# A two-layer decoder on one core: the MLP's second product in seven block products per 512 inner features, with half of the weight sums made in DRAM

## The chip, the core and the metric

The kernel runs on one NeuronCore of a Trainium2 chip. The metric is the device time of one execution in microseconds (us); lower is better. PE is TensorE (PEld its weight loads), DVE VectorE, ACT ScalarE, POOL GpSimd, SP SyncE. SP, ACT and POOL can issue DMAs; here SP issues nearly all of them.

## The reference

Two layers on x of 512 tokens x 1024 features, all in float32. A layer:

```
h = RMSNorm(x); z = h @ W_in                       # 1024 x 5888: attention, retention and gate columns
y = sigmoid(ga) * (attention @ W_a) + sigmoid(gb) * (retention @ W_b)
x = x + y @ W_out                                  # all of this is called mixing below
x = x + relu(RMSNorm(x) @ W_up)^2 @ W_down         # the MLP: 1024 -> 4096 -> 1024
```

A final RMSNorm follows. The change touches the MLP: `up` (512 tokens x 1024 times 1024 x 4096), the square of the ReLU, and `down` (512 x 4096 times 4096 x 1024).

## The kernel before

**Numbers.** Each float32 operand is split into a rounded `hi` (float32r, an ACT copy) and the rest `lo` (a DVE subtraction); a product is three matmuls, hi x hi, hi x lo, lo x hi (`products`, lines 274 to 282). Activations live with features on the 128 partitions and 512 tokens along the row; weights are the stationary operand, 128x128, and 512 tokens (in the pairs below 256) move.

**Weights.** All weights pass in a fixed order of units of 128x1024 (`unit_order`). `load_until` has SP fetch a unit into `raw` (three buffers), `split_until` makes `hi` and `lo` (three buffers each) and `unit` hands a unit out after it has split up to two more and loaded three ahead. So the buffers set the pace: the `hi` of unit i needs the end of unit i-3 on PE.

**MLP.** The first 512 inner features come from a plain `group` of four banks. The other 3584 come from 14 `pair`s of 256 inner features, each with a block scheme of seven products instead of eight (Strassen's, in Winograd's form): inputs are cut by feature half and token half, the sums of input blocks (`sums`) are made once per layer (`sum_input`), the sums of the weight blocks on DVE in `add_part` (four of 128x512 per pair), and a product is 12 matmuls of 256 columns. The banks a, e, b of a pair are chained: ACT copies a into b, b goes on accumulating, and so on. `rms_mlp.value`, the inverse root mean square per token, is multiplied in when a bank is read. z is squared and split to `hi` and `lo`.

**Order in the MLP** (`mlp_sequence`): the group, then two pairs, then in turn a down product and a pair. Inner features come in four quarters of 1024; a down product (`two_chunks`) is 256 output features from one quarter, two banks, 48 matmuls of 512 columns, added to x by DVE (`put_down`). The last quarter is done as a group and chunks, in layer 1 (`end`) in two halves of 256 tokens, so that the final norm of the first half runs beside the second. After layer 0 `put_down` also prepares the next layer's input (`scaled_input` makes `xh` and `xl`, `squared_input` the squares) and stores x to `spill`.

The order of instructions on each engine is made by the language's scheduler, which may move independent instructions past each other; each engine then runs its list strictly in order.

Of the kernel before, what the change touches and what calls it, by code (L numbers as in the profile page):

```python
# [10 lines left out]
F32 = mybir.dt.float32  # L11
# [32 lines left out]
N_IN = 46  # L44
UNIT = 1024
# [3 lines left out]
DELAY = 2  # L49


def unit_order():

    order = [("w_in", i) for i in range(4 + 2 + 8 + 2 + 4 + 2)]
    order += [("w_in", i) for i in range(22, 26)]
    order += [("w_a", i) for i in range(4)]
    order += [("w_in", i) for i in range(26, 42)]
    order += [("w_b", i) for i in range(4)]
    order += [("w_in", i) for i in range(42, 46)]
    order += [("w_b", i) for i in range(4, 8)]  # L60
    order += [("w_out", i) for i in range(8)]
    for what, q, i in mlp_sequence():
        if what == "first":
            order += [("w_up", u) for u in range(4)]
        elif what == "pair":
            order += [("pair", 8 * q + 2 * i, part) for part in range(4)]
        elif what == "down":
            order += [("w_down", 8 * q + 2 * i + u) for u in range(2)]
        else:
            order += [("w_down", 8 * q + u) for u in range(8)]  # L70
    return order


def mlp_sequence():

    seq = [("first", 0, 0), ("pair", 0, 2), ("pair", 0, 3)]
    for q in range(3):
        for i in range(4):  # L80
            seq += [("down", q, i), ("pair", q + 1, i)]
    return seq + [("last", 3, 0)]
# [32 lines left out]
def decoder(ctx, tc, xT, x_first, w_in, w_a, w_b, w_out, w_up, w_down, tables, decay, band, out):  # L115
# [14 lines left out]
    def temp(name="t"):  # L130
        return tmp.tile([P, T], F32, tag="t", name=name)
# [23 lines left out]
    raws, parts, homes = {}, {}, []  # L155
# [6 lines left out]
    def raw_tile():  # L162
        return wpool.tile([P, UNIT], F32, tag="raw", name="raw")

# [7 lines left out]
    def load_until(n):  # L172
        while state["loaded"] < min(n, len(order)):
            i = state["loaded"]
            layer, name, j = order[i][:3]
            if name == "pair":
                load_part(i)
            else:
# [12 lines left out]

    def load_part(i):
        layer, _, j, part = order[i]
        if part == 0:
            raws[i] = raw_tile()
            nc.sync.dma_start(raws[i][:, LEFT], w_up[layer, j][:, LEFT])
            raws[i + 3] = raw_tile()
            nc.sync.dma_start(raws[i + 3], w_up[layer, j + 1])
        elif part == 1:
            raws[i] = big("raw2").rearrange("p a t -> p (a t)")  # L200
            nc.sync.dma_start(raws[i][:, RIGHT], w_up[layer, j][:, RIGHT])

    def add_part(i):
        part = order[i][3]
        if part == 0:
            w2 = raws[i + 3]
            nc.vector.tensor_tensor(raws[i][:, RIGHT], w2[:, RIGHT], w2[:, LEFT], ALU.add)
        elif part == 1:
            w1 = raws[i - 1]
            nc.vector.tensor_tensor(raws[i][:, LEFT], w1[:, RIGHT], w1[:, LEFT], ALU.subtract)  # L210
        elif part == 2:
            raws[i] = big("raw3").rearrange("p a t -> p (a t)")
            w1, w2, z2 = raws[i - 2], raws[i + 1], raws[i - 1]
            nc.vector.tensor_tensor(raws[i][:, LEFT], w1[:, LEFT], w2[:, RIGHT], ALU.subtract)
            nc.vector.tensor_tensor(raws[i][:, RIGHT], z2[:, RIGHT], z2[:, LEFT], ALU.subtract)

    def split_until(n):
        while state["split"] < min(n, len(order)):
            i = state["split"]
            load_until(i + 3)  # L220
            paired = order[i][1] == "pair"
            if paired:
                add_part(i)
            raw = raws[i]
            if homes and i >= len(order) - len(homes):
                home = homes[len(order) - 1 - i]
                hi, lo = (home[:, 2 * a : 2 * a + 2, :].rearrange("p a t -> p (a t)") for a in range(2))
            else:
                hi = wpool.tile([P, UNIT], F32R, tag="hi", name="hi")
                lo = wpool.tile([P, UNIT], F32R, tag="lo", name="lo")  # L230
            for at in (LEFT,) if paired and order[i][3] == 3 else halves(i):
# [5 lines left out]
            raws.pop(i - 3 if paired else i, None)  # L237
# [117 lines left out]

    def square_sum(acc, src, first):
# [46 lines left out]
    def end(layer, uT):  # L403
        homes.extend(slots.four()[0] for _ in range(5))
        units = []
        H = T // 2
        g_last = 2 * DEPTH * KD

        def unit_at(i):
            if len(units) == i:  # L410
                units.append(unit("w_down", layer))
            return units[i]

        def half_products(ps, i, col, moving, at, start, stop):
            hi, lo = unit_at(i)
            cols = slice(col, col + P)
            products(ps, [((hi[:, cols], lo[:, cols]), tuple(m[:, at] for m in moving))], start, stop)

        class Half:
            def __init__(self, at):  # L420
                self.at = at
                self.acc = tmp.tile([P, T], F32, tag="acc", name="acc", bufs=1)[:, :H]

            def put(self, c, ps):
                xa = x[:, c, self.at]
                nc.vector.tensor_tensor(xa, xa, ps, ALU.add)
                if c == 0:
                    nc.scalar.activation(self.acc, xa, AF.Square)
                else:
                    sq = temp("sq")[:, :H]  # L430
                    nc.scalar.activation(sq, xa, AF.Square)
                    if c < KD - 1:
                        nc.vector.tensor_tensor(self.acc, self.acc, sq, ALU.add)
                    else:
                        self.last = sq
                nc.scalar.activation(xa, xa, AF.Copy, scale=gain[:, g_last + c : g_last + c + 1])

            def sums(self, ps, src, start):
                nc.tensor.matmul(ps, f32(ones), src, start=start, stop=not start)

            def gemm(self, meanwhile=None):
                banks = [bank(ps_mm, "mm")[:, :H] for _ in range(4)]
                for k in range(KD):
                    for c, ps in enumerate(banks):
                        half_products(ps, k // 2, (k % 2) * T + c * P, uT[k], self.at, k == 0, k == KD - 1)
                    if k == 1 and meanwhile:
                        meanwhile()
                for c, ps in enumerate(banks):
                    self.put(c, ps)
                for c in range(4, KD):  # L450
                    ps = bank(ps_mm, "mm")[:, :H]
                    for k in range(KD):
                        half_products(ps, c, k * P, uT[k], self.at, k == 0, k == KD - 1)
                    if c == KD - 1:
                        self.ssq = bank(ps_aux, "ssq")[:, :H]
                        self.sums(self.ssq, self.acc, True)
                    self.put(c, ps)

            def finish(self):
                self.sums(self.ssq, self.last, False)  # L460
                rstd = tmp.tile([P, T], F32, tag="rstd", name="rstd", bufs=2)[:, :H]
                nc.scalar.activation(rstd, self.ssq, AF.Sqrt, bias=eps, scale=1.0 / D)
                nc.vector.reciprocal(rstd, rstd)
                for k in range(KD):
                    if k % 2 == 0:
                        o = temp("o").rearrange("p (c t) -> p c t", t=H)
                    nc.vector.tensor_tensor(o[:, k % 2, :], x[:, k, self.at], rstd, ALU.mult)
                    if k in (0, 1, KD - 2, KD - 1):
                        nc.sync.dma_start(out[:, k, self.at], o[:, k % 2, :])
                    elif k % 2:  # L470
                        nc.sync.dma_start(out[:, k - 1 : k + 1, self.at], o)

        first = Half(slice(0, H))
        first.gemm()
        second = Half(slice(H, T))
        second.gemm(first.finish)
        second.finish()


    def layer_body(layer):  # L480
        g_mix, g_mlp = 2 * layer, 2 * layer + 1
        rms_mix, rms_mlp = Rms(g_mix), Rms(g_mlp)
# [94 lines left out]
        def put_q(c):  # L577
# [18 lines left out]
            {0: squares, 1: stats_first} if layer == 0 else {0: rms_mix.prepare, 1: stats},  # L596
# [103 lines left out]
        def gate(dest):  # L700
            def put(ps):
                nc.vector.tensor_tensor(dest, ps, rstd(), ALU.mult)
                nc.scalar.activation(dest, dest, AF.Sigmoid)

            return put
# [3 lines left out]
        def put_gate(c):  # L709
            def put(ps):  # L710
                nc.vector.tensor_tensor(mixed[c], ps, rstd(), ALU.mult)

# [9 lines left out]
        def put_ret(box, h):  # L722
            def put(ps):
# [4 lines left out]
                box[h] = (hi, lo)  # L728

# [524 lines left out]
```

## Time and profile before

| | |
|---|---|
| device time, median of 3 runs | 1511.3 us (1511.27 to 1512.82) |
| span of the profiled execution | 1511.4 us |
| busy in it: PE, PEld, DVE, ACT, POOL | 99%, 86%, 68%, 49%, 0% |
| DMA | 155.10 MB, mean 103 GB/s |
| MLP of layer 0, of layer 1 | about 414 to 751 us, 1161 to 1503 us with the final norm |

The profile is one execution seen by the hardware profiler. Part 1 of its page is the busy time of each engine, part 4 the chain of work that ended last. A group's row reads: line, engine, operation, output <- input, shape, count | busy us, mean ns of one | idle time just before them and what ended it. Matmuls are pipelined: one starts before the last has ended, so the mean of one is longer than the distance between two. A row of the table by stretches reads: from:to, length, then busy us (count) of PE, PEld, DVE, ACT, POOL, then the granted clock of PE, the DMA engines' share and GB/s.

### The profile page before, as it was taken

What the parts mean: (1) busy time and instruction counts of PE and PEld (TensorE: products, weight loads), DVE (VectorE), ACT (ScalarE), POOL (GpSimd) and SP (SyncE); (2) the same over time, 40 slices, a digit from 0 to 9 for tenths busy, and PEclk for the clock granted to TensorE, in tenths of its full rate; (3) what the DMA queues carried; (4) which work ended last, traced back from release to release, by engine and by line L of the source; (5) the groups of instructions that cost most, each with busy time, mean ns of one, the idle gap of its engine ahead of it and who ended that gap; (6) DMA issues with size and microseconds to landing.
All of it is one profiled execution on the core that took longest, in us unless ns stands there. A gap on an engine that the chain in (4) does not pass through costs nothing.

```text
span 1511.4 us, 20498 instructions
## 1 busy us (share of the span) xinstructions
PE 1499.2 (99%) x8080; PEld 1302.2 (86%) x8080; DVE 1026.7 (68%) x1598; ACT 740.1 (49%) x1163; POOL 2.9 (0%) x13
## 2 busy tenths in 40 slices
PE   9999999999999999999999999999999999999997
PEld 7888888888888999989888888888888999889997
DVE  6877668754787666676678765777449866666664
ACT  6656455632564444444455742555327544444452
POOL 0000000000000000000000000000000000000000
PEclk9999999999999999999999999999999999999999
DMA  6422322233223232233442222222342232232331
GB/s 217 123 97 75 98 79 91 70 125 126 98 78 104 98 112 97 93 104 115 165 131 93 84 84 98 82 79 84 126 125 98 85 104 92 99 111 98 103 108 56
DMA packets 52640, 155.10 MB, mean 103 GB/s; under 512 B 6208, under 2 KB 8384, under 8 KB 52544
## 3 DMA queue, kind: packets, MB, share of 16 engines
q1 hardware_dynamic: 52400, 153.54, 30.6%
q8 instruction: 63, 1.03, 0.3%
q14 instruction: 33, 0.27, 0.1%
q10 hardware_dynamic: 144, 0.26, 0.0%
HBM read 146.96 MB, written 4.19 MB: 100 GB/s over the span
## 4 chain that ended last, share of the span: by engine, by line
PE 98%; ACT 1%; DVE 0%; DMA 0%; issue 0%; DVEq 0%
PE mm L280 29%; PE mm L281 29%; PE mm L282 29%; PE rv L280 2%; PE rv L281 2%; PE rv L282 2%; PE score L651 1%; PE pT L616 1%; PE r L281 1%; PE r L282 1%; PE r L280 1%; PE pv L637 0%; PE pv L636 0%; PE ssq L374 0%; PE ret L281 0%; PE ret L282 0%
## 5 line engine op out<-in xcount | busy, mean ns | idle before, releaser
L235 ACT ACTIVATE hi<-raw 128x1024 fp32r<-128x1024 f32 (+1 forms) x313 | 314.6, 1013 | 517.9 <-PE mm L281 430.6
L236 DVE TENSOR_TENSOR lo<-raw,hi 128x1024 fp32r<-128x1024 f32 (+1 forms) x314 | 362.6, 1164 | 162.0 <-ACT hi L235 161.1
L281 PE MATMUL mm<-r,hi 128*128 128x512 f32 (+1 forms) x1136 | 392.5, 346 | 0.0
L280 PE MATMUL mm<-r,hi 128*128 128x512 f32 (+1 forms) x1136 | 389.5, 346 | 1.0 <-ACT mm L1037 1.0
L282 PE MATMUL mm<-r,lo 128*128 128x512 f32 (+1 forms) x1136 | 388.5, 346 | 0.0
L280 PE MATMUL mm<-xh,hi 128*128 128x512 f32 (+1 forms) x1008 | 358.2, 357 | 0.9 <-ACT xh L290 0.9
L281 PE MATMUL mm<-xl,hi 128*128 128x512 f32 (+1 forms) x1008 | 356.8, 356 | 0.0
L282 PE MATMUL mm<-xh,lo 128*128 128x512 f32 (+1 forms) x1008 | 355.4, 356 | 0.0
L280 PEld LDWEIGHTS mm<-r,hi 128*128 128x128 f32 x1136 | 214.8, 189 | 27.8 <-ACT mm L1037 1.4
L281 PEld LDWEIGHTS mm<-r,hi 128*128 128x128 f32 x1136 | 215.3, 189 | 26.3
L282 PEld LDWEIGHTS mm<-r,lo 128*128 128x128 f32 x1136 | 215.0, 189 | 25.7
L280 PEld LDWEIGHTS mm<-xh,hi 128*128 128x128 f32 x1008 | 191.1, 190 | 27.1 <-ACT xh L290 1.6
L281 PEld LDWEIGHTS mm<-xl,hi 128*128 128x128 f32 x1008 | 191.3, 190 | 25.5
L282 PEld LDWEIGHTS mm<-xh,lo 128*128 128x128 f32 x1008 | 191.0, 190 | 25.5
L1064 DVE TENSOR_TENSOR x<-x,mm 128x512 f32<-128x512 f32 x56 | 37.8, 687 | 34.2 <-PE mm L282 34.2
L282 PE MATMUL rv<-hi,xl 128*128 128x512 f32 x128 | 49.8, 389 | 0.0
L281 PE MATMUL rv<-lo,xh 128*128 128x512 f32 x128 | 49.8, 389 | 0.0
L280 PE MATMUL rv<-hi,xh 128*128 128x512 f32 x128 | 49.4, 391 | 0.0
L281 PE MATMUL mm<-ulo,hi 128*128 128x512 f32 (+1 forms) x128 | 46.3, 363 | 0.0
L280 PE MATMUL mm<-uhi,hi 128*128 128x512 f32 (+1 forms) x128 | 46.2, 362 | 0.0
L282 PE MATMUL mm<-uhi,lo 128*128 128x512 f32 (+1 forms) x128 | 45.7, 365 | 0.0
L1044 DVE SCALAR_TENSOR_TENSOR z<-mm,rstd 128x256 f32<-128x256 f32 x28 | 11.9, 425 | 42.0 <-PE mm L282 42.0
(188 smaller groups left out, 1682.1 us busy)
## 6 DMA issues: line engine op xcount, KB each, us to landing
raw<-w_in_in SPq DMA_DIRECT2D x89, 512.0 KB, 3.3
raw<-w_down_in SPq DMA_DIRECT2D x64, 512.0 KB, 3.3
raw<-w_up_in SPq DMA_DIRECT2D x36, 512.0 KB, 3.3
raw<-w_up_in SPq DMA_DIRECT2D x56, 256.0 KB, 2.7
raw<-w_b_in SPq DMA_DIRECT2D x16, 512.0 KB, 3.2
raw<-w_out_in SPq DMA_DIRECT2D x16, 512.0 KB, 3.5
raw<-w_a_in SPq DMA_DIRECT2D x8, 512.0 KB, 3.3
x<-xT_in SPq DMA_DIRECT2D x15, 256.0 KB, 3.6
```

The lines of the kernel that those rows point to most:

```text
L235: nc.scalar.activation(hi[:, at], raw[:, at], AF.Copy)
L236: nc.vector.tensor_tensor(lo[:, at], raw[:, at], f32(hi[:, at]), ALU.subtract)
L280: nc.tensor.matmul(ps, ah, bh, start=start and i == 0, stop=False, **more)
L281: nc.tensor.matmul(ps, ah, bl, start=False, stop=False, **more)
L282: nc.tensor.matmul(ps, al, bh, start=False, stop=stop and i == n - 1, **more)
L616: nc.tensor.transpose(pt[:, i * P : (i + 1) * P], sm[:, at : at + P], ident)
L651: nc.tensor.matmul(ps[:, g * w : (g + 1) * w], q_s[g][:, c, at], part[:, keys], start=i == 0, stop=i == 1)
L1044: nc.vector.scalar_tensor_tensor(z[:, 0, :H], a, 0.0, rms_mlp.value[:, :H], ALU.max, ALU.mult)
L1064: nc.vector.tensor_tensor(x[:, c, :], x[:, c, :], ps, ALU.add)
```

## The change

**The down product.** The MLP now goes in eight blocks e of 512 inner features: the group (e = 0) or two pairs, and straight after it `down(e)`, which does 512 tokens x 512 inner by 512 inner x 1024 with the same seven-product scheme. Its operands change places: z is the stationary operand (128 tokens at a time), the weights move, 512 columns. A product is 2 token blocks x 2 x 3 = 12 matmuls of 512 columns, and takes one weight unit (D0 to D6 in the text below). Banks a and c are in `ps_mm`, b in `ps_aux`; ACT copies a to b (2 x 512), then c and b out to SBUF (`p5`, `u2`) as they are needed again. The sums of z blocks (`u_forms`: four of 128x512 on DVE, split by ACT and DVE) need both pairs of the block, the first one (`one`) and D0 only the first pair.

**Its result.** It comes with tokens on the partitions. Each of eight 128x512 results of a block is put to SBUF and stored to `y` in DRAM by a DMA from POOL, in blocks 1 to 6 an accumulating one. In block 7 (`Ending`) y is read back, scaled by `factor`, the inverse mean square per token (so the norm's factor moves out of the pairs: relu(r a)^2 = r^2 relu(a)^2), and added. In layer 0 it is then turned by 32 PE transposes and added to x; the last quarter of that is carried into layer 1's first group, whose statistics come one unit later. In layer 1 x is turned to y's layout instead (32 transposes), and norm and output are done there.

**The weight sums.** Of the sums of weight blocks half are made on DVE (two of 512 per pair, two of 1024 per down block), the others in DRAM while mixing: POOL copies a part of the weights to `sums_up` or `sums_down` and, one step later, adds another part with an accumulating DMA. A step comes at every second of 48 places in mixing (`pace`), behind a tiny POOL copy of what was just made. SP then loads the sums like weights. A pair's units come in five loads of 256 KB, a down block's seven units in five of 512 KB.

**Buffers.** `raw` has six buffers and is loaded five units ahead (three and three before), `hi` and `lo` keep three; the 128x512 temporaries have seven instead of six, and the y results and bank copies share them. The scratch area for POOL's DMAs is set to 2048.

```diff
 N_IN = 46
+N_BLOCK = 8
+N_PAIR = 14
+AHEAD = 5
...
+    for e in range(N_BLOCK):
+        if e == 0:
             order += [("w_up", u) for u in range(4)]
         else:
-            order += [("w_down", 8 * q + u) for u in range(8)]
+            order += [("pair", 2 * e - 2 + i, part) for i in range(2) for part in range(4)]
+        order += [("block", e, part) for part in range(7)]
...
+    def sum_steps(layer):
...
+        for job in jobs + [None]:
+            if job:
+                to, source, n = job
+                nc.gpsimd.dma_start(to, source[:, :n])
+            if last:
+                to, source, n = last
+                nc.gpsimd.dma_start(to, source[:, n // 2 : n // 2 + n], accum_op=ALU.add)
+            last = job
+            yield
...
+        def down(e):
+            def multiply(ps, moving, start=True):
+                hi, lo = unit("block", layer)
+                for m in range(2):
+                    at = slice(m * P, (m + 1) * P)
+                    pairs = []
+                    for k, (uh, ul) in enumerate(moving):
+                        cols = slice(k * T, (k + 1) * T)
+                        pairs.append(((uh[:, at], ul[:, at]), (hi[:, cols], lo[:, cols])))
+                    products(ps[m], pairs, start, True, not start)
...
+            multiply(a, b11)
+            for m in range(2):
+                nc.scalar.activation(b[m], a[m], AF.Copy)
+            multiply(c, u_forms[0])
+            for m in range(2):
+                nc.scalar.activation(p5[m], c[m], AF.Copy)
+            multiply(b, u_forms[1], False)
+            for m in range(2):
+                nc.scalar.activation(u2[m], b[m], AF.Copy)
+            sink.begin(0)
+            multiply(a, b21, False)
+            for m in range(2):
+                sink.put(0, 0, m, a[m], 1)
+            sink.begin(1)
+            multiply(b, u_forms[2], False)
...
+            multiply(c, b22, False)
...
+            multiply(b, u_forms[3], False)
...
+                how = {"accum_op": ALU.add} if self.e else {}
+                nc.gpsimd.dma_start(y[:, 2 * j + m, i * T : (i + 1) * T], t, **how)
...
+        for e in range(N_BLOCK):
+            if e == 0:
+                group("w_up", layer, xs, [put_up(c) for c in range(4)], first_hooks())
             else:
+                pair()
+                pair()
+            down(e)
```

In the prediction the products of `down` are named by their units: D0 a = b11, D1 c = first sum, D2 b = second sum, D3 a = b21 (from `u_two`, the split of the second pair's z), D4 b = third sum, D5 c = b22, D6 b = fourth sum; A0 to A3 and B0 to B3 are the units of the block's two pairs.

More of the change, by code (lines that the diff above doesn't have):

```diff
@@ L177, in load_until @@
                 load_part(i)
+            elif name == "block":
+                load_block(i)
             else:
@@ L192, in load_part, with pace @@
+    DONE, steps = object(), []
+    pace_count = [0]
+    def pace(src):
+        pace_count[0] += 1
+        if steps and pace_count[0] % 2 == 0:
+            mark = small.tile([P, 1], F32, tag="mark", name="mark", bufs=2)
+            ins = nc.gpsimd.tensor_copy(mark, src[:, 0:1])
+            with tc.issue_after(ins.ins):
+                if next(steps[0], DONE) is DONE:
+                    steps.pop(0)
     def load_part(i):
         layer, _, j, part = order[i]
+        source, sums = w_pair[layer, j], sums_up[layer][j]
+        H = UNIT // 2
+        raws[i] = raw = raw_tile()
@@ L203, in add_part @@
-    def add_part(i):
-        part = order[i][3]
[L205 to L215, printed above, removed]
+            nc.sync.dma_start(raw[:, RIGHT], source[:, 3 * H :])
+        elif part == 2:
+            nc.sync.dma_start(raw[:, LEFT], sums[:, LEFT])
+        else:
+            nc.sync.dma_start(raw[:, LEFT], source[:, 2 * H : 3 * H])
@@ new lines, in add_part, with load_block @@
+    def add_part(i):
+        if order[i][3] in (1, 2):
+            last = raws.pop(i - 1)
+            at = LEFT if order[i][3] == 1 else RIGHT
+            nc.vector.tensor_tensor(raws[i][:, at], last[:, LEFT], last[:, RIGHT], ALU.add)
+    def load_block(i):
+        layer, _, e, part = order[i]
+        if part in (2, 5):
+            return
+        raws[i] = raw = raw_tile()
+        source, at = {
+            0: (w_down[layer, e], 0),
+            1: (sums_down[layer][e], 1),
+            3: (w_down[layer, e], 3),
+            4: (sums_down[layer][e], 0),
+            6: (w_down[layer, e], 2),
+        }[part]
+        nc.sync.dma_start(raw, source[:, at * UNIT : (at + 1) * UNIT])
@@ L219, in split_until @@
             i = state["split"]
-            load_until(i + 3)
-            paired = order[i][1] == "pair"
-            if paired:
+            load_until(i + AHEAD)
+            name, part = order[i][1], order[i][-1]
+            if name == "pair":
                 add_part(i)
+            elif name == "block":
+                add_block(i)
             raw = raws[i]
[L225 to L231, printed above, removed]
+            hi = wpool.tile([P, UNIT], F32R, tag="hi", name="hi")
+            lo = wpool.tile([P, UNIT], F32R, tag="lo", name="lo")
+            for at in (LEFT,) if name == "pair" and part == 3 else halves(i):
                 if i == 0 and at.start == 0:
@@ L236, in split_until @@
                 nc.vector.tensor_tensor(lo[:, at], raw[:, at], f32(hi[:, at]), ALU.subtract)
-            raws.pop(i - 3 if paired else i, None)
+            if not (name == "pair" and part < 2 or name == "block" and part < 4):
+                raws.pop(i)
             parts[i] = (hi, lo)
@@ L400, in finish @@
             inverse_rms(self.parts, D, self.value)
[L403 to L477, printed above, removed]
@@ L728, in put @@
                 box[h] = (hi, lo)
+                pace(f32(view(hi)))
             return put
@@ L755, in values @@
                 rv[pair, b] = (hi, lo)
+                pace(f32(view(hi)))
         rg, rg_next = {}, {}
@@ L969, in layer_body, with column_factors @@
             slots.give(*ms.pop(k))
-        H = T // 2
-        sums = [slots.four() for _ in range(4)]
-        by_form = [t[0].rearrange("p a (b t) -> p (a b) t", t=H) for t in sums]
+        last = layer == DEPTH - 1
+        sums = Forms((0, 2))
+        u_forms = Forms((0,))
+        u_two, u_two_slots = slots.four()
+        u_one = [slots.one() for _ in range(2)]
+        first_hi, first_lo = (view(t).rearrange("p (a t) -> p a t", t=H) for t in u_one)
+        columns = small.tile([P, 2 * NB], F32, tag="columns", name="columns", bufs=1)
+        factor, negative = columns[:, :NB], columns[:, NB:]
+        def column_factors():
+            ps = bank(ps_aux, "ssq")
+            acc = acc_of.pop(g_mlp)
+            for b in range(NB):
+                nc.tensor.matmul(ps[:, b : b + 1], acc[:, b * P : (b + 1) * P], f32(ones)[:, 0:1], start=True, stop=True)
+            nc.vector.tensor_scalar(factor, ps[:, :NB], 1.0 / D, EPS, ALU.mult, ALU.add)
+            nc.vector.reciprocal(factor, factor)
+            nc.vector.tensor_scalar(negative, factor, -1.0, None, ALU.mult)
+            return ps
         def sum_input(ks):
@@ L1060, in pair @@
[L1060 to L1070 removed]
+            multiply(b, part, True, sums[3], False)
+            nc.scalar.activation(z[:, 1, :H], b, AF.Relu, scale=-1.0)
@@ L1072, in first_hooks, with at0 @@
         def first_hooks():
+            used = []
+            def at0():
+                used.append(column_factors())
+                sum_input(0)
             def at1():
[L1074 removed]
+                nc.tensor.matmul(used[0], ones, xh[:, 0, :], start=True, stop=True)
                 sum_input(2)
[L1077 to L1097 removed]
```

339 lines of the change are left out of this document (229 added, 110 removed).

## The prediction

> **What bounds the kernel now.** First the page, part 1 (busy time) and part 4 (the chain that ended last), then its costliest group on ScalarE (ACT), then the busy times of 263 us of layer 0's MLP:
>
> ```profile
> span 1511.4 us, 20498 instructions
> ...
> PE 1499.2 (99%) x8080; PEld 1302.2 (86%) x8080; DVE 1026.7 (68%) x1598; ACT 740.1 (49%) x1163; POOL 2.9 (0%) x13
> ...
> PE 98%; ACT 1%; DVE 0%; DMA 0%; issue 0%; DVEq 0%
> ...
> L235 ACT ACTIVATE hi<-raw 128x1024 fp32r<-128x1024 f32 (+1 forms) x313 | 314.6, 1013 | 517.9 <-PE mm L281 430.6
> ```
> ```profile
> 437.00:700.00 263.00, 262.48 (x1672) 239.21 (x1671) 179.73 (x246) 121.13 (x173) 0.93 (x1) 1.00 0.30 100
> ```
>
> TensorE (PE) is the bound: 1499.2 of 1511.4 us, 98% of the chain. In those 263 us of the MLP it is busy for 262.5, DVE for 179.7 (68%), ACT for 121.1 (46%), at full granted clock (1.00). The L235 row tells how weights arrive: ACT rounds unit i to `hi`, and its idle time was ended by a matmul for 430.6 us, because `hi` has three buffers and unit i takes that of unit i-3: ACT waits for PE, not the other way. Where ACT is late, PE does stop; the list of PE's waits and the timeline show the one place in each layer's MLP:
>
> ```profile
> PE mm L280 <- ACT mm L1037: 1.0, 2, 0.5
> ```
> ```profile
> 437.56 0.28 PE L280 MATMUL mm<-r,hi 128*128 128x256 f32 x1
> ...
> 438.88 0.28 PE L282 MATMUL mm<-r,lo 128*128 128x256 f32 x1
> 439.68 0.39 PE L280 MATMUL mm<-r,hi 128*128 128x256 f32 x1 [0.52 <-ACT mm L1037]
> ```
> ```profile
> 520.00 0.39 PE L280 MATMUL mm<-r,hi 128*128 128x512 f32 x1
> ...
> 522.72 0.39 PE L280 MATMUL mm<-r,hi 128*128 128x512 f32 x1
> ```
>
> A duration of a matmul is not its pace. From 437.56 to 438.88 are 11 matmuls of 256 columns: 0.12 us each. From 520.00 to 522.72 are 12 of 512: 0.227 each. A product's result is there 0.16 us after its last pace (0.28 - 0.12). At 439 PE stood for 0.7 us because one ACT copy of a bank came late: the model of what follows.
>
> **Part 1: matmuls removed.** The second product had 32 x 8 x 3 = 768 matmuls of 512 columns in a layer, but layer 1's last quarter (192) ran as 384 of 256: 1344 x 0.227 + 384 x 0.12 = 351.2 us in both layers. Seven products instead of eight, 12 matmuls each, eight blocks, two layers: 1344 x 0.227 = 305.1 us. All on PE: **-46.1 us**.
>
> **Part 2: transposes.** 32 of 128x128 in each layer (the last block's `turn` and `add_x`).
>
> ```profile
> 84.94 0.60 PE L616 MATMUL pT<-ident,sm 128*128 128x128 f32 x4
> ```
>
> Four take 0.60 us, of which 0.28 is one's own: 0.11 each. 64 x 0.11 = **+7 us**.
>
> **Part 3: work on DVE and ACT.** Durations by shape:
>
> ```profile
> L236 DVE TENSOR_TENSOR lo<-raw,hi 128x1024 fp32r<-128x1024 f32 x280 | 339.9, 1222 | 138.2 <-ACT hi L235 137.3
> L235 ACT ACTIVATE hi<-raw 128x1024 fp32r<-128x1024 f32 x280 | 293.9, 1058 | 497.9 <-PE mm L281 410.6 <-issue 64.4 <-PE rv L282 14.5
> ...
> L1057 ACT ACTIVATE z<-z 128x512 f32<-128x512 f32 x56 | 35.0, 625 | 6.3 <-DVE z L1053 6.3
> ...
> L1053 DVE SCALAR_TENSOR_TENSOR z<-z,rstd 128x512 f32<-128x512 f32 x28 | 19.4, 693 | 1.0
> ...
> L207 DVE TENSOR_TENSOR raw<-raw 128x512 f32<-128x512 f32 x28 | 19.3, 688 | 8.9 <-DMA raw<-w_up_in 8.9
> ...
> L1049 DVE TENSOR_TENSOR z<-mm,eu 128x256 f32<-128x256 f32 x28 | 11.7, 418 | 0.0
> ...
> L1037 ACT ACTIVATE mm<-mm 128x256 f32<-128x256 f32 x28 | 10.3, 368 | 29.3 <-PE mm L282 29.3
> ```
>
> A block of the changed kernel is two pairs (168 matmuls x 0.12 = 20.2 us) and a down product (84 x 0.227 = 19.1): 39.2 us of PE. DVE in it: 13 `lo` of 1024 and two of 512 (17.3), four weight sums of 512 and two of 1024 (5.2), four 256-wide sums of z (1.7), four sums of u (2.8), splits of u, three of 512 and two of 1024 (4.5), four sums of results (2.8): 34.2 us, 87%. ACT: 13 + 2 `hi` (15.0), ten of 256 (3.7), two ReLU (1.3), two squares of 1024 (2.1), splits of u (4.0), ten bank copies (6.2): 32.3 us, 82%. Each still fits beside PE. Nearly full engines in fixed order cost PE time only where a product waits for a chain on them, and there is such a place.
>
> **Part 4: the stall in each block.** In the built program the scheduler has put the second pair's last product (call it B3) behind the first down product D0, then D1, then D3, D2, D5, D4, D6 (D3 is the second product into bank a, D2 the one with the second sum of u). On ACT, between B3 and D3, stands:
>
> ```
> hi of unit D2 (buffer of B3's unit: waits for B3's end) | copy a->b, 2nd bank | hi of unit D3
> ReLU of B3's result | square of z, 128x1024 | copy of D1's banks, 2 x 512 | hi of u_two, 128x1024 (D3 waits for it)
> ```
>
> ACT's pace when nothing is waited for is shorter than the durations above:
>
> ```profile
> 436.23 0.62 ACT L287 ACTIVATE r<-up 128x512 fp32r<-128x512 f32 x1
> 436.75 1.04 ACT L235 ACTIVATE hi<-raw 128x1024 fp32r<-128x1024 f32 x1
> 437.70 0.61 ACT L1010 ACTIVATE up<-up 128x512 f32<-128x512 f32 x1
> ```
>
> 0.52 for 512, 0.95 for 1024. From B3's end: 0.16 + 0.95 + 0.52 + 0.95 + 0.37 + 1.06 (needs the ReLU, so whole) + 2 x 0.52 + 1.06 + 0.1 (to PE) = 6.2 us. PE has only D1 meanwhile, 12 x 0.227 = 2.7: it stands for **3.5 us**. Then D2 needs the hi of the second sum, which ACT makes behind u_two's and one more weight `hi`: 2 x 0.95 + 0.62 = 2.52 after u_two's began, while PE went on 1.06 after that and has four matmuls (0.91): 0.55. Then D5 needs its `hi`, whose buffer D2 holds, and D5 stands directly behind D2: 0.16 + 1.06 + 0.13 = 1.35. Two shorter ones (D3's second half behind the `lo` of u_two; D4 behind a copy of D2's bank) about 0.1 each. Sum **5.6 us a block**, blocks 1 to 6 of both layers: 12 x 5.6 = **+67 us**. Nothing hides it: the cover of before was that pairs ran ahead of their down products by two, so that no product waited for a fresh z; now z is used at once, and PE's order is fixed.
>
> Block 0: the down product now follows the group directly, where two pairs stood before. Bank 1 of the group is ready 1.2 us before the group's end (six matmuls less 0.16); ReLU to -0.6, square to 0.5, a weight `hi` 0.95, hi of u 0.62: D0 starts 2.1 us late. Then 0.4 and 0.2 at D3 and D2, 1.35 at D5, 0.4 of small ones: 4.5 a layer, **+9**. Block 7: the same 5.6, plus eight scalings on ACT (layer 0) or twenty sums on DVE (layer 1): 7 a layer, **+14**.
>
> **Part 5: junction and tail.** Layer 1's first group now starts with `xh` and `xl` made after the last turns: after the last product's first half DVE has two sums of y (1.4), four of x (2.8), a `lo` (1.2) and `xl` (0.75) = 6.3 with 0.16 before it; PE has 14 transposes (1.5), half a product (1.4) and four matmuls (0.9): **+2.5**. The tail now:
>
> ```profile
> 1502.06 0.70 PE L439 MATMUL ssq<-sq,ones 128*128 128x256 f32 x2 [0.53 <-ACT sq L431]
> ...
> 1503.31 1.75 DVE L463 RECIPROCAL rstd<-rstd 128x256 f32<-128x256 f32 x1 [1.75 <-ACT rstd L462]
> ...
> 1507.70 0.93 SPq L469 DMA_DIRECT2D y_out<-o  x2
> ```
>
> PE ends at 1502.8, the span at 1511.4: 8.6 us. After: two sums (1.5), squares and roots (1.5), up to eight scalings of 512 (5.6), a store as now (3 after its issue): 12.6. **+4**.
>
> **Part 6: DMAs, cost taken as nothing.** POOL gets 44 weight-sum DMAs a layer in the mixing stage (a copy, one step later the accumulate, behind a 128x1 `mark` copy per step) and 56 stores of y, 48 of them accumulating; the trace has no POOL-issued and no accumulating DMA.
>
> ```profile
> q1 hardware_dynamic: 52400, 153.54, 30.6%
> ...
> raw<-w_up_in SPq DMA_DIRECT2D x56, 256.0 KB, 2.7
> ...
> dm<-decay_in SPq DMA_DIRECT2D x8, 256.0 KB, 3.7
> ```
> ```profile
> 10.00:12.00 2.00, 2.00 (x10) 1.64 (x10) 2.00 (x4) 2.00 (x5) 0.00 (x0) 1.00 1.05 402
> ```
>
> Lower bound: nothing, as moved bytes. The queues moved 402 GB/s at a full share. A block has 5.2 MB of loads and 8 x 0.26 MB of y, counted three times (read, read, write) 6.3 MB: 11.5 MB / 402 = 29 us, under 45. Mixing: 15.7 MB of sums, copied and accumulated, are 31 MB written (78 us at that rate) or 79 MB with all reads (196 us). The time for it:
>
> ```profile
> L711 DVE TENSOR_TENSOR x<-mm,rstd x16: 680/691/692, 48.1 to 839.8; 128x512 f32<-128x512 f32 x16
> ...
> L702 DVE TENSOR_TENSOR gb<-mm,rstd x16: 682/684/692, 290.6 to 1093.7; 128x512 f32<-128x512 f32 x16
> ```
> ```profile
> L1009 DVE SCALAR_TENSOR_TENSOR up<-mm,rstd x8: 691/692/692, 434.3 to 1181.2; 128x512 f32<-128x512 f32 x8
> ```
>
> A layer is 1181.2 - 434.3 = 747 us at most, so the steps run from the first gate (48) to the last (1094 - 747 = 347): 300 us, where the loads take 30%: 56% to 95% in all, hidden by the five units of lookahead. Three queues gain a wait. On SP a load of sums waits for its accumulate, and every later weight load stands behind it; block 0's sums are the first made, a whole stage earlier. SP's loads of y for block 7 wait for block 6's stores, issued two pairs (20 us) and more before. On ACT the first pair's bank copy takes one of seven buffers, which the second y store of the block before has to have left; 9.6 us lie between, and all of ACT stands behind it. No gain is possible: PE waited for no DMA before. Upper bound: the accumulates go in series, each as three transfers of 3.7 us, 11 us; eight are 89 us a block. I take nothing, since the nearest row (2.7 us for 256 KB) is under a third of those 9.6 us. By the Trainium skill's page "DMA: Bandwidth & Descriptors", section "Anatomy of one DMA", a GpSimd-issued DMA takes about 2.0 us plus its bytes over 436 GB/s, an estimated 2.6 us for 256 KB; in series eight of them are 21 us a block, also hidden. No run here shows it.
>
> **Sum**, against the profiled execution (1511.4, the median of the runs is 1511.3): -46.1 + 7 + 67 + 9 + 14 + 2.5 + 4 = +57.4, so **1569 us**. The sizes of the stalls (4 to 7 us a block) make it 1540 to 1600.
>
> **Rivals.**
> - *The stalls do not arise* (faster). Place: ACT between B3 and D3. If its chain ran within D1's 2.7 us, only D5's 1.35 would stay: -46.1 + 7 + 14 x 1.35 + 2 x 2.1 (block 0's start) + 6.5 = -9.5, 1502 us. It decides at (46.1 - 7 - 6.5) / 14 = 2.3 us a block: below, the change pays. For it: ACT had slack throughout. Against: the order in the program, the three `hi` buffers. Chance 0.18.
> - *The clock falls in the stalls.*
>
> ```profile
> 1504.00:1505.00 1.00, 0.00 (x0) 0.00 (x0) 1.00 (x1) 0.00 (x0) 0.00 (x0) 1.00 0.00 0
> 1505.00:1506.00 1.00, 0.00 (x0) 0.00 (x0) 0.96 (x4) 0.00 (x0) 0.00 (x0) 0.52 0.00 0
> ```
>
> At the end PE stops at 1502.8 and the clock is halved at 1505.0, after 2.2 us. A stall of 3.5 us may reach that; with half speed for as long as the stall, 1.75 us x 14 = 25: 1594 us. Chance 0.10. The Trainium skill's page "TensorE: Matmul & The Clock Gate", Part 1, has the clock fall only after an idle window of some 3.4 us, free-running, so a stall of 3.5 would rarely hold a whole one: an estimate of 1 us in all. The trace's 2.2 us is shorter, with sparse matmuls before it.
> - *POOL's DMAs queue up.* From 5.6 us an accumulate in series (45 / 8) they set the block: at 8 us, 64 a block, 12 x 19 = 228 more: about 1800. Chance 0.08.
> - *Nothing changes*, stalls eat exactly the gain: 0.02.
>
> **How the numbers follow.** Forecast (stalls as walked) 0.62. Slower by over 0.2% (3 us, about what a measurement can tell): 0.62 + 0.10 + 0.08 = 0.80; faster 0.18; same 0.02. Range: down to 1500, so that half of the faster case is in; up to 1612, with the clock case and without POOL's. Some 0.09 lies below and 0.10 above.
>
> **What would show it.** Part 1: matmul records down by some 5%, PE busy share in the MLP stage under 90%. Part 4: PE's waits named `hi` or ACT's r (u_two) with some 3.5 us, 14 times; a wait for `hi` of 1.35 behind D2; a block every 45 us. Part 3: DVE about 77%, ACT about 72% in the stage. Part 6: no PE wait for `raw`, and ACT's waits for y's DMAs near zero. Wrong if a block lasts under 42 us, or if PE's long waits name DMAs.

## The result, and the profile after

The changed kernel takes 1552.0 us (median of 4 runs, 1549.8 to 1553.2) against 1511.3: a ratio of 1.0266 (95% interval 1.0252 to 1.0281). The profiled execution has a span of 1551.4 us, 40.0 more than the one of before. The forecast of 1569 had the sign right and was 17 us too high; what follows shows that this is a difference of two larger errors.

The page of the changed kernel, parts 1 and 4, and its row for the same 263 us of layer 0's MLP as before:

```profile
span 1551.4 us, 21097 instructions
...
PE 1488.0 (96%) x7766; PEld 1267.4 (82%) x7766; DVE 1108.5 (71%) x1622; ACT 900.0 (58%) x1429; POOL 172.5 (11%) x261
...
PE 66%; issue 18%; DMA 4%; DVE 4%; ACT 4%; POOL 2%; DVEq 0%; ACTq 0%; SPq 0%; POOLq 0%
```
```profile
437.00:700.00 263.00, 247.73 (x1528) 218.45 (x1527) 196.53 (x232) 178.89 (x271) 39.71 (x48) 0.99 0.62 168
```

PE's share of the chain fell from 98 to 66%, and in the MLP PE is busy for 247.7 of 263 us instead of 262.5. DVE is at 75%, ACT at 68% (77 and 72 were forecast). For whom PE waits:

```profile
PE mm L321 <- ACT r L328: 27.0, 16, 1.9
PE mm L323 <- DVE lo L276: 8.9, 8, 2.3
PE mm L321 <- ACT mm L1063: 3.6, 4, 1.7
PE b L321 <- ACT r L328: 3.5, 13, 0.3
PE mm L321 <- ACT xh L331: 2.3, 2, 1.8
```

The first row is D3's wait for `u_two` (14 blocks) with D0's in block 0 (twice); the fourth is D2's for the second sum; the second and third are first pairs of blocks. Such rows understate a wait, as a matmul's row lasts longer than its pace (0.39 against 0.227 us). So I count start to start, less the paces of 0.227, 0.12 and 0.11 us, from 416 us to PE's end (1502.8 and 1537.7):

| PE's lost time, us | before | after |
|---|---|---|
| D3 in 14 blocks, D0 in block 0 | | 29.6 |
| D2 | | 5.7 |
| inside stretches at half clock | | 12.2 |
| first pairs, waiting for DVE `lo` or ACT's bank copy | 1.4 | 14.8 |
| junction of the layers | | 2.6 |
| others, and gaps under 0.15 | 4.6 | 14.3 |
| sum | 6.0 | 79.2 |

With -46.1 for the products, +7.0 for the transposes, 16 small matmuls of `column_factors` (1.8), 73.2 of stops, 0.5 from layer 0's mixing and 5.0 of tail that is +41.4, against 40.0 measured.

**D3's wait.** The timeline of block 2, from D0's last matmul on (lines of the changed kernel: L275 makes a weight's `hi`, L1079 is the ReLU of B3's result, L328 the `hi` of `u_two`):

```profile
523.61 0.39 PE L323 MATMUL mm<-hi,r 128*128 128x512 f32 x1
523.84 0.28 PE L321 MATMUL mm<-r,hi 128*128 128x256 f32 x1
...
524.09 1.06 ACT L275 ACTIVATE hi<-raw 128x1024 fp32r<-128x1024 f32 x1 [0.62 <-PE mm L323]
...
525.05 0.58 ACT L1105 ACTIVATE b<-mm 128x512 f32<-128x512 f32 x1
525.15 0.28 PE L323 MATMUL mm<-r,lo 128*128 128x256 f32 x1
...
525.27 0.63 PE L321 MATMUL mm<-hi,r 128*128 128x512 f32 x2
525.57 1.04 ACT L275 ACTIVATE hi<-raw 128x1024 fp32r<-128x1024 f32 x1
...
526.51 0.37 ACT L1079 ACTIVATE z<-mm 128x256 f32<-128x256 f32 x1
...
526.91 1.06 ACT L1026 ACTIVATE z<-z 128x1024 f32<-128x1024 f32 x1
...
527.80 0.39 PE L323 MATMUL mm<-hi,r 128*128 128x512 f32 x1
527.88 1.07 ACT L1108 ACTIVATE eu<-mm 128x512 f32<-128x512 f32 x2
...
528.83 1.06 ACT L328 ACTIVATE r<-z 128x1024 fp32r<-128x1024 f32 x1
...
529.94 0.50 PE L321 MATMUL mm<-hi,r 128*128 128x512 f32 x1 [1.76 <-ACT r L328]
```

B3 starts at 523.84 and ends at 525.27, D1 runs to 528.03, D3 starts at 529.94: 1.92 us late, from a chain of 4.67 us. ACT's order is the one that the prediction listed, link for link. But the `hi` of D2 starts at 524.09, 1.18 us before B3 ends, released by D0's last matmul. (Which `hi` is whose is read from the built program, where the one of D2 has D0's buffer and the one of D3 has B3's; the times alone would also fit the two changed about.) It took D0's buffer, since D0 stands ahead of B3 on PE: the buffers go on in the order in which PE leaves them, not "unit i from unit i-3", as the text ahead of the result has it. From the ReLU (526.51) to D3 are 3.43 us, 3.6 in the prediction. D5's wait is missing for the same reason; its `hi` takes D3's buffer, not D2's, and is done half a microsecond ahead of D5:

```profile
535.58 0.39 PE L323 MATMUL mm<-hi,r 128*128 128x512 f32 x1
...
536.00 1.06 ACT L275 ACTIVATE hi<-raw 128x1024 fp32r<-128x1024 f32 x1 [3.70 <-PE mm L323]
...
537.64 0.62 PE L321 MATMUL mm<-hi,r 128*128 128x512 f32 x2
```

A block, from D3 to D3, lasts 43.6 us (six of them from 486.66 to 748.19), against 39.2 of work on PE:

```profile
486.66 0.50 PE L321 MATMUL mm<-hi,r 128*128 128x512 f32 x1 [1.75 <-ACT r L328]
```
```profile
748.19 0.50 PE L321 MATMUL mm<-hi,r 128*128 128x512 f32 x1 [1.75 <-ACT r L328]
```

**The clock.** Two pairs of neighbouring stretches of 3.41 us; the first of each pair holds a D3 wait (the granted clock is the third number from the right):

```profile
527.89:531.30 3.41, 1.49 (x6) 0.67 (x4) 3.41 (x6) 3.41 (x7) 0.00 (x0) 1.00 0.23 77
531.30:534.72 3.42, 3.31 (x8) 2.64 (x9) 3.42 (x4) 1.00 (x2) 0.00 (x0) 0.50 0.04 10
572.26:575.67 3.41, 1.96 (x7) 1.33 (x8) 3.41 (x6) 3.41 (x5) 0.00 (x0) 1.00 0.26 77
575.67:579.09 3.42, 3.42 (x16) 2.63 (x16) 3.05 (x4) 1.17 (x3) 0.00 (x0) 1.00 0.17 53
```

The same wait of 1.92 us is followed by 3.4 us at half clock at 531 and not at 575. By starts and paces PE was busy for 0.30 of the first stretch and 0.45 of the third. The MLP stages have eight such stretches (the expectations below were written with a count of seven), all whole multiples of 3.41 us apart: five behind a D3 wait, one behind D0's in block 0, two behind first pairs. PE was busy for 0.27 to 0.39 of the stretch before each. Stretches on the same grid at 0.39 (from 1429.0) and 0.40 (from 702.0 and 766.8) were followed by full clock, so in this trace the line lies near 0.39; how sharp it is stays open.

**The first pairs.** End of block 1:

```profile
500.61 0.69 DVE L1144 TENSOR_TENSOR y<-mm,eu 128x512 f32<-128x512 f32 x1 [0.64 <-DMA y<-y]
...
502.09 1.09 ACT L1142 ACTIVATE y<-b 128x512 f32<-128x512 f32 x2 [2.49 <-DMA y<-y]
...
502.49 0.38 PE L323 MATMUL mm<-xh,lo 128*128 128x256 f32 x1 [1.00 <-DVE lo L276]
```
```profile
ACT y L1142 <- DMA y<-y: 32.8, 11, 3.8
```
```profile
y<-y POOLq DMA_DIRECT2D x112, 256.0 KB, 7.3
```

D6's results and a sum wait for a temporary that an earlier store of y still reads; the store lands 7.3 us after its issue. Behind them in ACT's and DVE's order stand the `hi`, `lo` and bank copies of the next block's first pair. DMA bandwidth is enough on average (share 0.62 above) but not where it is wanted:

```profile
528.00:538.00 10.00, 7.97 (x27) 5.99 (x27) 8.12 (x10) 6.01 (x9) 0.00 (x0) 0.83 0.16 52
538.00:548.00 10.00, 10.00 (x55) 8.52 (x54) 7.10 (x9) 6.68 (x10) 5.62 (x8) 1.00 0.86 173
548.00:558.00 10.00, 10.00 (x86) 10.00 (x85) 5.64 (x7) 5.18 (x10) 1.44 (x2) 1.00 1.08 274
```

All eight stores of a block are issued within ten us, here from 539.3 to 547.8. In the twenty us from 538 on the DMA engines are close to full (shares of 0.86 and 1.08), at 173 and 274 GB/s, below the 402 GB/s of the reading stretch in the prediction.

### The profile page after: what moved, and what is told of

It is laid out like the page before. It is cut to its first block, busy times and chain, and to the rows that moved or that the text cites. A ratio compares the mean times of both kernels' runs of the same rounds, so it can differ in the third digit from the quotient of the medians.

```text
span 1551.4 us, 21097 instructions
## 1 busy us (share of the span) xinstructions
PE 1488.0 (96%) x7766; PEld 1267.4 (82%) x7766; DVE 1108.5 (71%) x1622; ACT 900.0 (58%) x1429; POOL 172.5 (11%) x261
## 4 chain that ended last, share of the span: by engine, by line
PE 66%; issue 18%; DMA 4%; DVE 4%; ACT 4%; POOL 2%; DVEq 0%; ACTq 0%; SPq 0%; POOLq 0%
PE mm L323 18%; PE mm L321 18%; PE mm L322 18%; DMA y<-y 3%; POOL y L1148 2%; PE rv L321 2%; PE rv L322 2%; PE rv L323 2%; ACT hi L275 1%; DVE lo L276 1%; DMA dm<-decay_in 1%; PE score L660 1%; PE b L321 1%; PE pT L625 1%; PE b L322 1%
## 5 line engine op out<-in xcount | busy, mean ns | idle before, releaser
L275 ACT ACTIVATE hi<-raw 128x1024 fp32r<-128x1024 f32 (+1 forms) x366 | 373.2, 1020 | 400.6 <-PE mm L322 251.2
L276 DVE TENSOR_TENSOR lo<-raw,hi 128x1024 fp32r<-128x1024 f32 (+1 forms) x367 | 428.0, 1171 | 200.5 <-ACT hi L275 199.2
L321 PE MATMUL mm<-r,hi 128*128 128x256 f32 (+1 forms) x768 | 252.7, 329 | 3.6 <-ACT mm L1063 3.6
L322 PE MATMUL mm<-r,hi 128*128 128x256 f32 (+1 forms) x768 | 252.0, 328 | 0.0
L323 PE MATMUL mm<-r,lo 128*128 128x256 f32 (+1 forms) x768 | 252.0, 328 | 0.0
L1148 POOL DMA_DIRECT2D y<-y x112 | 93.6, 997 | 660.4 <-ACT y L1142 612.8
L321 PEld LDWEIGHTS mm<-r,hi 128*128 128x128 f32 x768 | 146.9, 191 | 17.8 <-ACT mm L1063 4.7
L322 PEld LDWEIGHTS mm<-r,hi 128*128 128x128 f32 x768 | 146.8, 191 | 12.8
L323 PEld LDWEIGHTS mm<-r,lo 128*128 128x128 f32 x768 | 146.8, 191 | 12.6
L321 PE MATMUL mm<-hi,r 128*128 128x512 f32 x256 | 96.8, 407 | 27.0 <-ACT r L328 27.0
L322 PE MATMUL mm<-lo,r 128*128 128x512 f32 x256 | 102.1, 399 | 0.0
L323 PE MATMUL mm<-hi,r 128*128 128x512 f32 x256 | 101.1, 407 | 0.8 <-DVE r L329 0.5
L321 PE MATMUL b<-hi,r 128*128 128x512 f32 x192 | 79.1, 412 | 4.7 <-ACT r L328 3.5
L322 PE MATMUL b<-lo,r 128*128 128x512 f32 x192 | 77.3, 402 | 0.0
L323 PE MATMUL b<-hi,r 128*128 128x512 f32 x192 | 72.3, 390 | 0.0
## 6 DMA issues: line engine op xcount, KB each, us to landing
sums_down<-w_down_in POOLq DMA_DIRECT2D x32, 1024.0 KB, 10.8
```

Of the source, the lines that this page charges most:

```text
L275: nc.scalar.activation(hi[:, at], raw[:, at], AF.Copy)
L276: nc.vector.tensor_tensor(lo[:, at], raw[:, at], f32(hi[:, at]), ALU.subtract)
L321: nc.tensor.matmul(ps, ah, bh, start=start and i == 0, stop=False, **more)
L322: nc.tensor.matmul(ps, ah, bl, start=False, stop=False, **more)
L323: nc.tensor.matmul(ps, al, bh, start=False, stop=stop and i == n - 1, **more)
L1148: nc.gpsimd.dma_start(y[:, 2 * j + m, i * T : (i + 1) * T], t, **how)
```

## The experiments

After this comparison the theory was: D3's wait is a chain over ACT with too little beside it; its windows at half clock and the late first pairs (temporaries held by accumulating stores) make up the rest. Rivals: ACT is short of time altogether; the half clock costs nothing because PE waits anyway; the first pairs are late by their loads, or by the weight sums.

**b3_first**: more work beside the chain.

```diff
-            multiply(b, part, True, sums[2], False)
+            end = multiply(b, part, True, sums[2], False)
...
+            if second:
+                with tc.issue_after(end.ins):
+                    multiply(e, part, False, block(1, 1), False)
...
+            if ends:
+                with tc.issue_after(ends[-1].ins):
+                    multiply(a, b11)
```

`second` marks a block's second pair, and `ends[-1]` is its last product, B3.

> B2's second product is put ahead of its first one on PE and B3 ahead of D0, all else left to the scheduler. Theory (the stall is the chain from B3's end to D3, with only D1 beside it): now D0 and D1, 5.5 us, lie beside a chain of 0.16 + half of D0 1.36 + copy 0.52 + square 1.06 + copy 0.52 + hi 0.95 + hi of u_two 1.06 + 0.1 = 5.7, so the wait at D3 falls from 1.9 to 0.2 to 0.5 us, 13 times, and the half-clock windows that follow it (5 of the 7 in the MLP) go: 21 + 8 = -25 to -31 us, 1521 to 1527. Rival (ACT is short of time in this part of the block, so that the wait only moves to D2, D4 or D5): under -8 us, 1544 or more.

1537.2 us (1532.9 to 1548.0; ratio to before 1.0176, 1.0136 to 1.0215). D3's wait fell from 1.92 to 0.38 us as the theory said: with D0's, PE's waits for ACT r fell from 27.0 to 6.7 us. But the time came down by 15 and not 25, outside both ranges. PE's waits now, in the slowest of the four executions (1548.0), which is the one that was profiled:

```profile
PE mm L321 <- ACT mm L1066: 24.6, 12, 2.8
PE mm L321 <- ACT r L329: 6.7, 15, 1.9
```

L1066 is the first pair's bank copy, behind ACT's copies to y. The wait did not move to D2, D4 or D5, so ACT was not short of time there; the second stop of the block took over (start to start 26.5 us at the bank copies in this trace).

**fill**: PE busy while it waits.

```diff
-            multiply(c, u_forms[0])
+            end = multiply(c, u_forms[0])
...
-            multiply(a, b21, False)
+            if e:
+                spare = bank(ps_aux, "fill")
+                with tc.issue_after(end.ins):
+                    for _ in range(6):
+                        more = nc.tensor.matmul(spare, ones, xh[:, 0, :], start=True, stop=True)
+                with tc.issue_after(more.ins):
+                    multiply(a, b21, False)
```

> Six matmuls of 512 columns on idle data go into a spare bank between D1 and D3 of blocks 1 to 7 (1.36 us, less than the 1.9 us that PE waits there); nothing of the computation is changed. Theory (a 3.4 us window in which PE was busy for under 0.39 is followed by one at half clock, and PE is the bound in it): the five half-clock windows behind D3's wait go, 1.7 us each: -6 to -9 us, 1543 to 1546, the wait at D3 itself as before. Rival (in those windows PE would have waited for ACT anyway): within 2 us of the changed kernel, 1550 to 1554.

1540.5 us (1538.7 to 1541.2), 11.5 less than the changed kernel, by nothing but useless matmuls.

```profile
PE mm L321 <- ACT r L329: 9.0, 15, 1.9
```

Of the 1.92 us at D3 the 0.56 that they don't fill are left, and up to the last block no stretch at half clock follows them any more, so the rival falls. The gain is larger than forecast, and under half of it lies in the stretches themselves: lost time at half clock fell from 12.2 to 7.4 us, that in first pairs from 14.8 to 7.1. Why the first pairs gained is not settled.

**no_sums**: no DMA of the weight sums while mixing.

> The weight sums are not made in DRAM: a part of the weights is loaded in place of each sum (so the MLP's values are not the reference's). Theory (the DRAM sums cost only the late decay tables of the mixing stage, 1.2 us in layer 0 and 0.9 in layer 1): -1 to -3 us, 1549 to 1551, the MLP as before. Rival (they also make the MLP's loads late): -8 us or more.

1549.9 us (1547.0 to 1551.5): -2, as the theory said, though the two kernels' runs overlap; the tables `dm` land after 3.7 us again, not 8.5. The rival's 8 us are not there. The late first pairs stay (11.3 us waiting for `lo`, 1.0 for the bank copy). Making the sums in DRAM costs little.

**y_big**: y's results in other buffers.

```diff
-                t = temp("y")
+                if m == 0:
+                    self.two = big("y")
+                t = self.two[:, m, :]
```

> The y results take halves of the 128x2x512 buffers, not the seven 128x512 temporaries that the bank copies use too. Theory (ACT's last copies of a block wait 3 us for a temporary that an accumulating store still reads, and all of ACT and so the next block's first pair are late by it): ACT's 33 us of waits for y's DMAs go, and most of the 15 us that PE loses in the first pairs, with the two half-clock windows there: -8 to -16 us, 1536 to 1544. Rival (the first pairs are late by the loads of raw): -3 to 0 us.

1595.0 us (1594.2 to 1597.8), 43 more: neither. ACT's waits for y's DMAs are gone, but with other buffers the scheduler chose another order on ACT and DVE at the block's end. DVE's sum of the next pair's weights (L236) stands there ahead of results and of `lo`, and waits some 3 us for its load in each block; PE waits behind it:

```profile
DVE raw L236 <- DMA raw<-sums_up: 44.5, 14, 4.0
```
```profile
PE mm L323 <- DVE lo L276: 36.7, 14, 3.4
```

So this run says nothing on the temporaries; the next two do it with PE's order kept.

**y_plain**: stores that don't accumulate.

```diff
-                how = {"accum_op": ALU.add} if self.e else {}
+                how = {}
```

> The stores of y in blocks 1 to 6 overwrite instead of accumulating (so the blocks' results are not summed, and the output isn't the reference's); the order on PE, ACT and DVE is that of the changed kernel. Theory (the accumulating stores fill the DMA engines for 20 us of each block, share 0.9 to 1.1, and so both the temporaries and the next loads of raw are late, which costs PE 15 us in the first pairs and two half-clock windows): most of that goes, -10 to -17 us, 1535 to 1542. Rival (it is POOL's issuing and the order of the queues, which stay): -4 to 0 us, 1548 or more.

1536.2 us (1532.7 to 1537.5): -15.9. Lost time in first pairs fell from 14.8 to 0.3, at half clock from 12.2 to 5.8, while D3's wait stayed. The same 256 KB land in 4.4 us at the median:

```profile
y<-y POOLq DMA_DIRECT2D x112, 256.0 KB, 4.4
```

**inplace**: fewer temporaries.

```diff
-                t = temp("y")
+                t = temp("y") if more is None else more
```

> The four y results that are sums overwrite the bank copies p5 and u2 that they are made of, so a block takes 10 of the seven temporaries' turns instead of 14; PE's order is that of the changed kernel. If ACT's 33 us of waits for temporaries are what makes the first pairs late: they shrink to under 10 us, and the time by -6 to -12 us, 1540 to 1546. If the late loads of raw are: -3 to +1 us.

1537.9 us (1533.1 to 1539.1): -14.1, with the accumulating stores and the loads as they were. Of ACT's 32.8 us of waits for y's DMAs this is left:

```profile
ACT y L1174 <- DMA y<-y: 0.7, 1, 0.7
```

The first pairs lose 3.7 instead of 14.8. So the link is the temporary, not the load. (D3's wait is the same 1.92 us in these two runs.)

**b3_inplace_t8**: both, and `bufs=8` for the temporaries.

> PE's order of b3_first with the in-place sums and one more temporary (eight). Theory (in b3_first the 26 us at the first pair's bank copies are ACT's waits for temporaries, the last thing that is late): they go, with the half-clock windows behind them, 7 x 1.7 at most: 1537 - 20 to 36, so 1501 to 1517, about the kernel before. Rival (the loads of raw, slowed by the accumulating stores, take their place): 1525 to 1537.

1515.3 us (1514.2 to 1517.5; ratio to before 1.0029, 1.0017 to 1.0040): -36.8, more than the two alone (15 and 14 make 29). That each stop had hidden part of the other fits this; but the eighth temporary is new here, and no run separates its share. What PE still waits for:

```profile
PE mm L321 <- ACT r L329: 6.6, 15, 1.9
PE mm L321 <- ACT xh L332: 3.4, 2, 2.8
PE mm L323 <- DVE lo L276: 2.3, 3, 1.8
```

**b3_group** and **b3_group_u2**: the rest of the waits for ACT r.

```diff
+            if name == "w_up" and u == 3:
+                turns = [(j, c) for two in (0, 2) for j in range(2) for c in (two, two + 1)]
...
-                split(u_two[:, 0:2, :], u_two[:, 2:4, :], z)
+                for at in (slice(0, H), slice(H, T)):
+                    split(u_two[:, 0:2, at], u_two[:, 2:4, at], z[:, :, at])
```

The first cut is in both, the second (from `split` on) in b3_group_u2 alone.

> b3_inplace_t8, and the last unit of the MLP's group runs banks 0 and 1 first, so that bank 1 is ready 12 matmuls before the group's end instead of 6. The wait at D0 of block 0 (2.05 us) falls by 6 x 0.227 = 1.36 to 0.7, and with it the half-clock window behind it goes (1.7): 2 x 3.1 = -6 us, 1515 to 1509, against 1511 of the kernel before. If the wait is set by something else than bank 1: 1515.

> As b3_group, and hi and lo of u_two are made in two halves of 256 tokens, since D3 reads only the first. If the 0.38 us at D3 and the 0.25 behind it are the chain through hi and lo of u_two (1.06 becomes 0.6), both go in 13 blocks: -6 to -8 us more, 1501 to 1503. If ACT and DVE lose as much by the two extra instructions: -2 to +2 against b3_group.

b3_group: 1509.8 us (1504.2 to 1512.4; ratio 0.9985, 0.9975 to 0.9994), where 1509 was expected; D0's wait in block 0 fell from 2.05 to 0.72. b3_group_u2: **1502.2 us** (1501.8 to 1502.9; ratio to before 0.9937, 0.9925 to 0.9949), inside its range and 0.6% faster than the kernel before: of the 46 us that the products save 9 are kept. Its page and PE's longest waits:

```profile
PE 1471.2 (98%) x7766; PEld 1262.1 (84%) x7766; DVE 1105.1 (74%) x1638; ACT 899.2 (60%) x1445; POOL 173.1 (12%) x261
```
```profile
PE mm L322 <- DVE lo L276: 5.0, 13, 0.5
PE mm L321 <- ACT xh L332: 3.4, 2, 2.8
```

D3 no longer waits for `u_two`; half a microsecond for a weight's `lo` has come in its place.

**fixed_rotation**: the prediction's reading of the buffers, made true.

```diff
-            hi = wpool.tile([P, UNIT], F32R, tag="hi", name="hi")
+            hi = wpool.tile([P, UNIT], F32R, tag=f"hi{i % 3}", name="hi", bufs=1)
```

(and `lo` likewise)

> The changed kernel with three hi and three lo buffers of their own names, unit i taking those of unit i-3 for certain; the scheduler then puts hi of D3 ahead of hi of D2 and D5 behind D4. If hi of D2 waits for B3's end as the prediction had it, its row starts 0.16 us after B3's last matmul and not 1.2 us before; with D3's hi already made, the wait at D3 stays near 1.9 us, D5 waits for nothing, and the time stays within 4 us of the changed kernel (1548 to 1556). If fixed buffers alone bring the prediction's 3.5 us at D3: 1572 or more.

1565.3 us (1563.0 to 1568.2), 13 more: outside both ranges. ACT's two `hi`, D3's and then D2's, now follow each other, the second one behind B3's end (525.77 is its last matmul):

```profile
525.15 2.00 ACT L275 ACTIVATE hi<-raw 128x1024 fp32r<-128x1024 f32 x2
```
```profile
525.77 0.28 PE L323 MATMUL mm<-r,lo 128*128 128x256 f32 x1
```

D3 waits for 1.84 us, no more than before, and D5 for nothing. What it costs lies in the first pairs, 21.0 us start to start for the bank copy, at the block's end, where ACT's order has changed too:

```profile
PE mm L321 <- ACT mm L1063: 19.1, 12, 2.2
```

So with fixed buffers the kernel is slower, but not by its waits at D3 or D5, where the prediction charged 2.5 us a block. Fixed buffers together with the order of the changed kernel, which is what the prediction had added up, were not run.

## Why the prediction was right or wrong

| step | on record, us | measured, us |
|---|---|---|
| products | -46.1 | -46.1 (384 fewer of 256 columns, at 0.12) |
| transposes | +7 | +7.0 |
| DVE and ACT each fit beside PE | 77%, 72% | 75%, 68% |
| D3 | 3.5 a block | 1.92 in 13 of 14, 0.54 in the last |
| D2 | 0.55 | 0.44 |
| D5 | 1.35 | 0 |
| block 0 | 4.5 a layer | 2.35 a layer |
| half clock | a rival (+25) | 12.2 |
| first pairs, DMAs | 0 | 13.4 more than before |
| mixing, decay tables late | 0 | 2 |
| junction, tail | +2.5, +4 | +2.6, +5.0 |

**Right:** the sign and its mechanism. Removing the lead of the pairs over the down products leaves D3 waiting for a chain over ACT in the listed order, and 46 us of matmuls don't pay for it. b3_first shows the cause: with D0 beside the chain too, the wait falls to 0.38 us.

**Wrong in size, in Part 4:** the step "hi of unit D2 (buffer of B3's unit: waits for B3's end)". It charged 1.1 us at D3 and 1.35 at D5 for buffers that were already free. The waits at D0, D2 and D3 of all blocks come to 35 us; for the blocks' stalls 67 + 9 + 14 = 90 were forecast.

**Wrong in Part 6:** "ACT's waits for y's DMAs near zero". They are 32.8 us, and inplace and y_plain show that these, through the temporaries, make the first pairs late. The argument compared 9.6 us with a landing of 2.7 us, a plain load at a quiet moment. The accumulating store takes 7.3 there, and the last copies of D6 ask for a temporary earlier than the next block's bank copy, for which the 9.6 us were counted. The Trainium skill's page "DMA: Bandwidth & Descriptors", section "Anatomy of one DMA", gave an estimated 2.6 us; y_plain's 4.4 and the accumulating 7.3 both stand above it, with DMA shares of 0.60 to 0.83 and of 0.86 to 1.08 in the twenty us from 538 on.

**Between forecast and rival:** the clock. I gave it 0.10 as a case of its own, with every stall paying. It happens in 8 places and costs 12.2 us. The Trainium skill's page "TensorE: Matmul & The Clock Gate", Part 1, has a free-running window of some 3.4 us, and the trace agrees with its length (3.41). Its condition, an idle window, asks for more than was needed here: a window busy for up to 0.39 was still followed by half clock.

These omissions (13, 12, 2 us and some 8 of small gaps) cancelled most of the overcharge of 55. That the forecast came within 17 us is in so far luck: two wrong terms of opposite sign. "PE busy under 90%" failed with it (94%), and "a block every 45 us" came out at 43.6.

## What to carry to other kernels

Before a wait is priced by a buffer, look up whose end actually releases it: with the pools here it was the next one that the consuming engine leaves, in that engine's program order. In these traces a stall cost more than its length where it emptied most of a stretch of 3.41 us, and its removal uncovered the next stop of the same block, so that fixes were worth more together (37 us, with one more buffer) than alone (15 and 14). Count a store's landing time, not its bytes, against the moment at which its source buffer is wanted again, and count it in the crowd of its own burst.

## What was not expected of the hardware

- Half clock after a window that was busy for 0.27 to 0.39, on a fixed grid of 3.41 us; waits of 1.92 us trigger it or not by where they fall on the grid.
- An accumulating store of 256 KB to DRAM lands 7.3 us after its issue at the median, the same store without accumulation (y_plain) 4.4 us. Copies and accumulates from DRAM to DRAM take 9.8 us (512 KB) and 10.8 us (1 MB) at the median.
- The Sqrt at the end costs ACT a table load of 1.28 us in the tail, between the last sums of squares and the output; I had counted the roots without it (part of the 5.0 us):

```profile
1540.19 1.28 ACT L1215 ACT_TABLE_LOAD   x1
```
